# A hybrid attention and state-space layer on one core: two more pairs of gate blocks by Strassen's rule, other filler places, later loads, and low weight parts by ScalarE and an adding DMA

## The chip, the cores and the metric

The kernel runs on one core of a Trainium2 chip. The metric is the device time of one execution in microseconds (us). Before the change the median of three runs is 1958.16 us (1956.68 to 1961.07).

## What is computed

One layer of a streaming encoder is applied to 1152 tokens: a prompt of 1024 and eight samples of 16. One wide input projection feeds two branches, and what matters here is this part of it:

```python
h = rms_norm(x, norm_g) * (1 + scale) + shift
proj = h @ w_in
q, k, v, z_att, z_ssd, xbc, dt_raw, gates = jnp.split(proj, IN_SPLITS, axis=-1)
...
y = (y + d_skip.astype(jnp.float32)[:, None] * xs_h).reshape(b, s, SSD_WIDTH).astype(x.dtype)
y = y * jax.nn.silu(z_ssd)
...
merged = jax.nn.sigmoid(g_att) * att_branch + jax.nn.sigmoid(g_ssd) * ssd_branch
out = x + gate * (merged @ w_out)
```

`z_ssd` has 2048 columns, that is 16 blocks of 128, one for each pair of state-space heads. `gates` has 16 blocks, `xbc` 24. The state-space scan (`ssd_scan`) works on 32 heads in four groups, in chunks.

## The kernel before

All products with weights are made in fp32r as three matmuls: a weight block is split into a high part (ScalarE copies it to fp32r, L372) and a low part (VectorE subtracts the high part from the raw block, L373), and `high*high + high*low + low*high` is accumulated (L487, L488, L490). One "dense block" is 128 output columns over 1024 inputs and 1152 tokens: 8 x 3 x 3 = 72 matmuls of 128x384. `dense` (L455) does one; its three token groups are evicted from PSUM one after the other, the first two out of the two buffers `d`, the third out of `s`. Each block's two parts take two of four slots in `rarena`, so the parts of block i+1 can be written once block i-1 is done. The raw weights come by a DMA on SyncE's queue (L348) into two raw slots.

The program has these stages, all on TensorE:

- the start: loads, modulation and norm, then the first dense blocks;
- Strassen: ten of the 16 z blocks are taken two at a time (`pairs`, L823). Two output blocks over two token halves and two input halves need seven products instead of eight: per pair 7 x 4 x 2 x 3 = 168 matmuls of 128x288 (L878, L880, L881). `NPR` = 5 is the number of pairs. The results go to DRAM (`z_d`);
- attention, eight units;
- the state-space stage: 24 convolution blocks of `xbc` (`conv_gen`, L1495), 11 other dense blocks between them (the fillers: five z blocks in the pairs 3, 5, 9, 11, 13, three gate blocks in the groups 1 to 3, three in the pairs 7, 14, 15), the scan of 16 pairs of heads (`ssd`, L1665), and six more gate blocks at its end (`gates_dense`);
- the tail: attention projection, state-space projection, output projection.

In the state-space stage the order of the instructions is made at build time by generators: `dense` blocks are issued while the steps of the scan are paced between them by a clock that the program keeps for itself. For pair p, `prelude` (L1708) loads the decays of its two heads (`acs_d`, two broadcasts of 576 KB), the exponentials `eacs_d` (two of 288 KB, into `eb`) and the state `h0`, and ScalarE turns the decays into masks (L1728, L1732). `main` (L1738) transposes x (L1755), makes the states (L1800), the output within the chunks (L1828, L1835) and from the states (L1856), multiplies by `eb` (L1861) and by z (L1869), and stores y through GpSimd's queue (L1873). A z block made early comes back from `z_d` in `main` (L1841). One that is made in the stage lies in SBUF from its eviction (L1698 on ScalarE, L1699 on VectorE) to L1869. The engines work in order; GpSimd's queue has the stores of the stage, memsets and copies for the convolution (L1498, L1501, L1517, L1518) and masks (L1789).

Of the kernel before, what the change touches and what calls it, by code (L numbers as in the profile page):

```python
# [18 lines left out]
NT = NP + NB * NS  # L19
G3 = NT // 3  # L20
NH = 16
HD = 64
NU = NH // 2
NPAIR = 16
NG = 4
PPG = NPAIR // NG
# [103 lines left out]
def trunk_kernel(ctx: ExitStack, tc: tile.TileContext, h):  # L130
    nc = tc.nc
# [4 lines left out]
    drp = ctx.enter_context(tc.tile_pool(name="drp", bufs=1, space=bass.MemoryType.DRAM))  # L136
# [30 lines left out]
    class Slots:  # L167
# [12 lines left out]
        def alloc(self, dtype):  # L180
            return Slot(self, self.free.pop(0), dtype)
# [35 lines left out]
    for n, w in PARAMS:  # L217
# [31 lines left out]
    L_SSD = marena.set_layout(Z0, [("X", 1, XW), ("R", 2, 1184), ("t", 8, 36), ("pad", 1, 576), ("T", 9, NT), ("Y", 1, 1184), ("H", 1, 1024),  # L249
                                  ("g", 3, G3)])  # L250
# [62 lines left out]
    store = nc.gpsimd.dma_start  # L313
# [8 lines left out]
    z_d = drp.tile([1 + len(EARLY), P, NT], F32, name="z_d")  # L322

    def rsqrt_small(v):

# [9 lines left out]
    jobs, parts = [], []  # L335
# [16 lines left out]
    def w_split(i, keep=lambda x: x, cold=None):  # L352

        n = len(jobs[i])
        if n == 2:
            raise NoSlot("pair")
        if n == 4:
            return w_split_last(i, keep)
        if i not in wsplit:
            lay = L_W3 if n == 3 else L_WA if jobs_att[0] <= i <= jobs_att[1] else L_W  # L360
            hi = alloc(lay, "w", n * 1024, cold)
            try:
                lo = alloc(lay, "w", n * 1024, cold)
# [8 lines left out]
        keep(nc.scalar.activation(hi.r[:, c], b.ap, AF.Copy))  # L372
        keep(nc.vector.tensor_tensor(lo.r[:, c], b.ap, hi.ap[:, c], ALU.subtract))  # L373
        b.free()
        wsplit[i][2] = j + 1
        w_ahead()
# [631 lines left out]

    def keep_block(n, z):
        what, i = AHEAD_BLOCKS[n - 1]  # L1010
        dma(gate_d[i] if what == "gate" else z_d[1 + EARLY.index(i)], z.ap)

    z = [alloc(L_VT, "T", NT)]
    w_done(0)
# [597 lines left out]

    ngate = [4]

    def gate_dense(**how):
        i = ngate[0]
        ngate[0] += 1

        def ev(o, g, tok, ps):
            t = yield from walloc(L_SSD, "g", G3)  # L1620
            nc.scalar.activation(t.ap, ps, AF.Tanh, scale=0.5)
            store(gate_d[i][:, tok], t.ap)
            stored(t)

        yield from dense(hops, ev, **how)
# [4 lines left out]
    def group_dense(g, lay):  # L1630
        res = grp[g] = {"b": [], "c": [], "sq": None, "st": None}
        yield from conv_gen(16 + g, lay, res["b"])
        if g:
            yield from gate_dense()
        yield from conv_gen(20 + g, lay, res["c"])

    def group_lat(g):
# [30 lines left out]
    def ssd(p):  # L1668
# [10 lines left out]
        def dense_gen():  # L1679
            res = st["x"] = []  # L1680
            lay = L_SSD if p else L_HEAD
            while p > AHEAD and not ssd_all[p - AHEAD]:
                blocked[0] = "pairs ahead"
                yield None
            if p % PPG:
                yield from conv_gen(p, lay, res)
            if p in EARLY:
                st["go"] = True
                if p % PPG == 0:
                    yield from conv_gen(p, lay, res)  # L1690
                if p in GATED:
                    yield from gate_dense()
                return
            z = yield from walloc(lay, "T", NT)
            st["go"] = True

            def evz(o, g_, tok, ps):
                nc.scalar.activation(z.ap[:, tok], ps, AF.Tanh, scale=0.5)  # L1698
                nc.vector.scalar_tensor_tensor(z.ap[:, tok], z.ap[:, tok], 1.0, ps, ALU.add, ALU.mult)  # L1699

            yield from dense(hops, evz)
            if p % PPG == 0:
                yield from conv_gen(p, lay, res)
            st["z"] = z
            if p in GATED:
                yield from gate_dense()

        def prelude():  # L1708

            yield from ready(lambda: "go" in st and "t" in dts and ssd_all[p] and "cbm" in grp[g])  # L1710
            res = grp[g]
            yield from until(dts["t"])
            me = []
            for hd in hds:
                a = yield from walloc(lay, "T", NT)
                dma(a.ap, acs_d[hd:hd + 1].to_broadcast([P, NT]))
                me.append(a)
            eb = yield from walloc(lay, "T", NT)
            for e in range(2):
                dma(eb.ap[e * HD:(e + 1) * HD], eacs_d[hds[e]:hds[e] + 1].to_broadcast([HD, NT]))  # L1720
            h0 = yield from walloc(lay, "H", NP)
            dma(h0.ap, h["h0"][p])
            yield from pause(7000)
            for e in range(2):

                for c in range(9):
                    cs = slice(c * P, (c + 1) * P)
                    nc.scalar.activation(me[e].ap[:, cs], me[e].ap[:, cs], AF.Relu, scale=-1.0,  # L1728
                                         bias=a4[:, c, hds[e]:hds[e] + 1])
                    if c % 3 == 2:  # L1730
                        yield from pause(1100)
                nc.scalar.activation(me[e].ap, me[e].ap, AF.Exp, scale=-1.0)  # L1732
# [3 lines left out]
            st["me"] = me, eb, h0, clock[0] + 1500  # L1736

        def main():  # L1738
            yield from ready(lambda: ssd_all[p] and ("z" in st or p in EARLY) and "cbm" in grp[g] and "t" in dts and st.get("x"))
            x, tx = st["x"][0]  # L1740
            res = grp[g]
            tokb, ct = res["tok"], res["ct"]
# [19 lines left out]
            me, eb, h0, tm = st["me"]  # L1762
            ssd_all[p + 1] = True

            if res["st"] is None:
# [73 lines left out]
            if p in EARLY:  # L1839
                z = alloc(lay, "T", NT)  # L1840
                dma(z.ap, z_d[1 + EARLY.index(p)])  # L1841
# [371 lines left out]
```

## Time and profile before

| what | value |
|---|---|
| median of three runs | 1958.16 us |
| profiled execution, its own time | 1957.76 us |
| its span, first to last instruction | 1955.9 us |
| VectorE busy | 1231.6 us, 63% |
| ScalarE busy | 794.4 us, 41% |
| GpSimd busy | 328.2 us, 17% |
| mean granted TensorE clock | 0.998 |

Times of the profile are of one execution. The windows view gives, for a stretch of it, how long each engine was busy and how many instructions it began. A matmul is pipelined, so TensorE can read as busy without a gap while matmuls begin twice as often as they last; what one costs is the stretch divided by its count. The waits view tells which engine sat idle before which line, and what ended that.

### The profile page before, as it was taken

To read this page: it belongs to the slowest core of one execution; us is meant where nothing else is said; L and a number is where in the kernel's file an instruction comes from. 1 tells how busy PE (TensorE), PEld (TensorE's weight loads), DVE (VectorE), ACT (ScalarE), POOL (GpSimd) and SP (SyncE) were. 2 spreads that over 40 slices of the span, in tenths; PEclk is the share of its full clock that TensorE was granted. 3 is DMA by queue.
4 is the path that set the end of the run, shared out by engine and by line. 5 is a ranking of instruction groups with operands and counts; after the bars stand their busy time and mean duration, and the time that the engine had idled before them with its cause. 6 is when DMAs were issued, how large, how long until landed. Compare 5 with 4: busy or idle time off the path is not lost. (4 is left out here: it accounts for less than half of the span.)

```text
span 1955.9 us, 35553 instructions
## 1 busy us (share of the span) xinstructions
PE 1931.8 (99%) x14211; PEld 1848.8 (95%) x14211; DVE 1231.6 (63%) x2545; ACT 794.4 (41%) x1627; POOL 328.2 (17%) x612
## 2 busy tenths in 40 slices
PE   7999999999999999999999999999999999999999
PEld 5999999998999998989999999989999999999999
DVE  7756346556555564585968768987775434777732
ACT  8433244444444444456545544655333301111200
POOL 0000032131231212210223322322322300000000
PEclk9999999999999999999999999999999999999999
DMA  8223423333333323234444444564357653331241
GB/s 317 88 80 105 178 68 94 128 115 96 122 103 113 121 95 117 80 121 118 129 132 131 147 129 148 155 187 147 93 177 271 234 192 92 104 104 56 84 144 53
DMA packets 84477, 252.82 MB, mean 129 GB/s; under 512 B 14540, under 2 KB 15576, under 8 KB 84312
## 3 DMA queue, kind: packets, MB, share of 16 engines
q1 hardware_dynamic: 76120, 224.26, 35.8%
q0 software_dynamic: 8192, 26.29, 3.5%
q8 instruction: 112, 1.84, 0.4%
q14 instruction: 53, 0.43, 0.1%
HBM read 199.78 MB, written 50.73 MB: 128 GB/s over the span
## 5 line engine op out<-in xcount | busy, mean ns | idle before, releaser
L487 PE MATMUL d<-rarena 128*128 128x384 f32 x1352 | 462.8, 342 | 5.7 <-DVE ma_att L1699 2.8
L490 PE MATMUL d<-rarena 128*128 128x384 f32 x1352 | 456.1, 337 | 0.0
L488 PE MATMUL d<-rarena 128*128 128x384 f32 x1352 | 455.7, 337 | 0.0
L487 PEld LDWEIGHTS d<-rarena 128*128 128x128 f32 x1352 | 254.8, 188 | 11.5 <-issue 3.7
L488 PEld LDWEIGHTS d<-rarena 128*128 128x128 f32 x1352 | 255.0, 189 | 1.2 <-issue 0.7
L490 PEld LDWEIGHTS d<-rarena 128*128 128x128 f32 x1352 | 254.6, 188 | 1.4 <-issue 1.1
L555 PE MATMUL d<-va_att,rarena 128*128 128x384 f32 (+1 forms) x567 | 197.6, 349 | 0.0
L553 PE MATMUL d<-va_att,rarena 128*128 128x384 f32 (+1 forms) x567 | 196.6, 347 | 0.0
L554 PE MATMUL d<-va_att,rarena 128*128 128x384 f32 (+1 forms) x567 | 193.7, 342 | 0.0
L372 ACT ACTIVATE rarena<-arena 128x1024 fp32r<-128x1024 f32 x80 | 84.7, 1059 | 268.0 <-PE s L488 175.7
L487 PE MATMUL s<-rarena 128*128 128x384 f32 x520 | 176.9, 340 | 0.0
L488 PE MATMUL s<-rarena 128*128 128x384 f32 x520 | 174.6, 336 | 0.0
L490 PE MATMUL s<-rarena 128*128 128x384 f32 x520 | 174.2, 335 | 0.0
L1297 ACT ACTIVATE ma_att<-ma_att 128x640 f32<-128x640 f32 (+2 forms) x144 | 101.5, 706 | 136.9 <-DVE ma_att L1406 99.7
L373 DVE TENSOR_TENSOR rarena<-arena,rarena 128x1024 fp32r<-128x1024 f32 x80 | 98.8, 1235 | 51.5 <-ACT rarena L372 51.3
L1226 POOL TENSOR_SCALAR ma_att<-ma_att 128x16 f32<-128x16 f32 (+1 forms) x24 | 5.2, 216 | 665.5 <-DVE ma_att L1203 664.8
L555 PEld LDWEIGHTS d<-va_att,rarena 128*128 128x128 f32 x567 | 107.1, 189 | 3.9 <-issue 2.7
L553 PEld LDWEIGHTS d<-va_att,rarena 128*128 128x128 f32 x567 | 106.8, 188 | 2.7 <-issue 1.2
L554 PEld LDWEIGHTS d<-va_att,rarena 128*128 128x128 f32 x567 | 106.8, 188 | 0.5
L487 PEld LDWEIGHTS s<-rarena 128*128 128x128 f32 x520 | 97.7, 188 | 2.2 <-issue 1.8
L1529 DVE SCALAR_TENSOR_TENSOR ma_att<-ma_att,arena 128x1176 f32<-128x1176 f32 x63 | 94.3, 1496 | 6.4 <-ACT ma_att L1526 5.9
L488 PEld LDWEIGHTS s<-rarena 128*128 128x128 f32 x520 | 97.7, 188 | 0.0
(436 smaller groups left out, 3914.9 us busy)
## 6 DMA issues: line engine op xcount, KB each, us to landing
arena<-in_wall_dram SPq DMA_DIRECT2D x85, 512.0 KB, 3.8
ma_att<-in_kc_dram SPq DMA_DIRECT2D x64, 256.0 KB, 4.5
ma_att<-in_vc_dram SPq DMA_DIRECT2D x64, 256.0 KB, 3.2
ma_att<-acs_d SPq DMA_DIRECT2D x26, 576.0 KB, 4.0
y_d<-ma_att POOLq DMA_DIRECT2D x15, 576.0 KB, 3.4
ma_att<-y_d SPq DMA_DIRECT2D x15, 576.0 KB, 4.8
arena<-in_wssd_dram SPq DMA_DIRECT2D x16, 512.0 KB, 4.5
ma_att<-eacs_d SPq DMA_DIRECT2D x24, 288.0 KB, 5.6
```

What stands on the lines that cost most here:

```text
L372: keep(nc.scalar.activation(hi.r[:, c], b.ap, AF.Copy))
L373: keep(nc.vector.tensor_tensor(lo.r[:, c], b.ap, hi.ap[:, c], ALU.subtract))
L487: nc.tensor.matmul(ps, hi.r[:, wc], kh.r[:, tok], start=k == 0, stop=False)
L488: nc.tensor.matmul(ps, hi.r[:, wc], kl.r[:, tok], start=False, stop=False)
L490: nc.tensor.matmul(ps, lo.r[:, wc], kh.r[:, tok], start=False, stop=k == nk - 1)
L553: nc.tensor.matmul(ps, kh.r[:, tok], wh, start=j == 0, stop=False)
L554: nc.tensor.matmul(ps, kh.r[:, tok], wl, start=False, stop=False)
L555: nc.tensor.matmul(ps, kl.r[:, tok], wh, start=False, stop=j == KT - 1)
L1226: nc.gpsimd.tensor_scalar(ss, ss, 1.0 / HD, EPS, ALU.mult, ALU.add)
L1297: nc.scalar.activation(p, p, AF.Exp, bias=sm_[:, 4 + e:5 + e], scale=-1.0, accum_out=sm_[:, 6 + e:7 + e])
L1529: nc.vector.scalar_tensor_tensor(yc, r.ap[:, j:j + n], w4[:, i, j:j + 1], yc, ALU.mult, ALU.add)
```

## The change

1. `NPR` goes from 5 to 7. Fourteen of the 16 z blocks (0 to 13) go by Strassen's rule, z block 14 is one dense block right after them (before, z block 15 was); all z now go through DRAM.
2. The fillers of the state-space stage are seven instead of eleven: z block 15 in pair 1, gate blocks in the pairs 3, 6, 9, 11, 13 and 15. `fill_dense` makes them; the groups have none. Six gate blocks stay at the stage's end.
3. `eb` is no longer loaded in `prelude` but in `main`, after the output within the chunks; z is loaded right behind it, for every pair. VectorE's multiplications wait for them (`until(te)`, `until(tz)`).
4. For the weight blocks of the state-space stage (from the first convolution block to the last gate block) the low part is made without VectorE: ScalarE writes the negated high part into the low slot (L375 of the changed file), and a DMA on GpSimd's queue adds the raw block from DRAM to it (L376). The blocks of the other stages go as before.

```diff
-GATED = (7, 14, 15)
-NGATE = 7 + len(GATED)
-EARLY = tuple(p for p in range(16) if p not in (3, 5, 9, 11, 13))
-AHEAD_BLOCKS = [("gate", i) for i in range(4)] + [("z", p) for p in EARLY]
+NEARLY = 15
+SLOTS = (('p', 1), ('p', 3), ('p', 6), ('p', 9), ('p', 11), ('p', 13), ('p', 15))
+AHEAD_BLOCKS = [("gate", i) for i in range(4)] + [("z", p) for p in range(NEARLY)]
...
-NPR = 5
+NPR = 7
...
         keep(nc.scalar.activation(hi.r[:, c], b.ap, AF.Copy))
-        keep(nc.vector.tensor_tensor(lo.r[:, c], b.ap, hi.ap[:, c], ALU.subtract))
+        if jobs_att[1] <= i < len(jobs) - 32:
+            keep(nc.scalar.activation(lo.r[:, c], hi.ap[:, c], AF.Copy, scale=-1.0))
+            keep(nc.gpsimd.dma_start(lo.r[:, c], parts[jobs[i][j]], accum_op=ALU.add))
+        else:
+            keep(nc.vector.tensor_tensor(lo.r[:, c], b.ap, hi.ap[:, c], ALU.subtract))
...
+    def fill_dense(*slot):
+        what, i = FILL[slot]
+        if what == "gate":
+            yield from gate_dense()
+            return
+
+        def ev(o, g, tok, ps):
+            t = yield from walloc(L_SSD, "g", G3)
+            nc.scalar.activation(t.ap, ps, AF.Tanh, scale=0.5)
+            nc.vector.scalar_tensor_tensor(t.ap, t.ap, 1.0, ps, ALU.add, ALU.mult)
+            store(z_d[1 + i][:, tok], t.ap)
+            stored(t)
+
+        yield from dense(hops, ev)
...
-            eb = yield from walloc(lay, "T", NT)
-            for e in range(2):
-                dma(eb.ap[e * HD:(e + 1) * HD], eacs_d[hds[e]:hds[e] + 1].to_broadcast([HD, NT]))
             h0 = yield from walloc(lay, "H", NP)
...
-            if p in EARLY:
-                z = alloc(lay, "T", NT)
-                dma(z.ap, z_d[1 + EARLY.index(p)])
-                tz = clock[0] + 6500
-            else:
-                z, tz = st["z"], 0.0
+            eb = alloc(lay, "T", NT)
+            for e in range(2):
+                dma(eb.ap[e * HD:(e + 1) * HD], eacs_d[hds[e]:hds[e] + 1].to_broadcast([HD, NT]))
+            z = alloc(lay, "T", NT)
+            dma(z.ap, z_d[1 + p])
+            te, tz = clock[0] + 6500, clock[0] + 8500
...
+                yield from until(te)
                 nc.vector.tensor_tensor(eb.ap[:, c2], eb.ap[:, c2], v, ALU.mult)
```

Three queues show what moves in the state-space stage. First ScalarE, before, in the middle of the stage: L372 is the high part of a weight block, L1506, L1509 and L1510 are the evictions of a convolution block, L1621 of a gate block, L1728 and L1732 the masks out of the decays.

```order
L1728 ACTIVATE ma_att<-ma_att 128x128 x18
L1732 ACTIVATE ma_att<-ma_att 128x1152 x2
L372 ACTIVATE rarena<-arena 128x1024
L1509 ACTIVATE ma_att<-s_13324 128x256
L1510 ACTIVATE ma_att<-s_13324 128x8x16
L1526 ACTIVATE ma_att<-ma_att,arena 128x1176
L1621 ACTIVATE ma_att<-d_13358 128x384
```

ScalarE in the changed kernel, at a like place (L373 is the high part, L375 the negated copy, L1511 the eviction of a convolution block, L1730 and L1734 the masks):

```order
L373 ACTIVATE rarena<-arena 128x1024
L1734 ACTIVATE ma_att<-ma_att 128x1152 x2
L1531 ACTIVATE ma_att<-ma_att,arena 128x1176
L1511 ACTIVATE ma_att<-d_13078 128x384
L1783 ACTIVATE rarena<-ma_att 64x128
L1730 ACTIVATE ma_att<-ma_att 128x128
L375 ACTIVATE rarena<-rarena 128x1024
L1730 ACTIVATE ma_att<-ma_att 128x128 x7
L1877 ACTIVATE va_ssd<-ma_att 128x1152
```

The negated copy is new, and it does not always follow its high part at once: here an eviction of the block that is running and a mask on a decay stand between the two. In most blocks one or two instructions do.

Next GpSimd's queue before, late in the stage (L1815 and L1899 store states, L1873 y, L1789 makes masks for the samples' state):

```order
L1498 MEMSET ma_att 128x3
L1501 COPY ma_att<-ma_att 128x8x3
L1815 DMA out_hp_dram<-ma_att 128x128
L1789 TENSOR_TENSOR rarena<-rarena,arena 128x256 x2
L1873 DMA y_d<-ma_att 128x1152
L1498 MEMSET ma_att 128x3
L1501 COPY ma_att<-ma_att 128x8x3
L1899 DMA out_hs_dram<-ma_att 128x1024
```

And in the changed kernel (L376 is the adding DMA, L1522 to L1524 the tails of a convolution block, L1876 stores y, L1902 the samples' states, L1817 the prompt's state):

```order
L376 DMA rarena<-in_wall_dram 128x1024
L1876 DMA y_d<-ma_att 128x1152
L1503 MEMSET ma_att 128x3
L1791 TENSOR_TENSOR rarena<-rarena,arena 128x256 x2
L1902 DMA out_hs_dram<-qa_ssd 128x1024
L1817 DMA out_hp_dram<-ma_att 128x128
L1522 COPY ma_att<-ma_att 128x3
L1523 COPY ma_att<-ma_att 128x24
L1524 DMA out_conv_dram<-ma_att 128x27
L376 DMA rarena<-in_wall_dram 128x1024
```

The adding DMA stands once per weight block in this queue, behind whatever is queued there, and mostly right behind the copies that follow the end of a convolution block; there are 34 of them.

Last SyncE's queue before, around one pair of heads (L1716 loads decays, L1720 `eb`, L1722 `h0`, L1841 z, L348 raw weights):

```order
L1722 DMA qa_ssd<-in_h_dram 128x1024
L1716 DMA ma_att<-acs_d 128x1152 x2
L1720 DMA ma_att<-eacs_d 64x1152 x2
L348 DMA arena<-in_wall_dram 128x1024
L1716 DMA ma_att<-acs_d 128x1152 x2
L1722 DMA ma_att<-in_h_dram 128x1024
L1720 DMA ma_att<-eacs_d 64x1152
L1841 DMA va_ssd<-z_d 128x1152
```

And in the changed kernel (L1721 loads decays, L1843 `eb`, L1724 `h0`, L1845 z, L349 raw weights):

```order
L1724 DMA ma_att<-in_h_dram 128x1024
L1721 DMA ma_att<-acs_d 128x1152
L349 DMA arena<-in_wall_dram 128x1024
L1843 DMA va_ssd<-eacs_d 64x1152 x2
L1845 DMA ma_att<-z_d 128x1152
L1721 DMA ma_att<-acs_d 128x1152
```

The loads of `eb` are now beside that of z, and the second of the two decays of a pair stands behind both.

More of the change, by code (lines that the diff above doesn't have):

```diff
@@ L31 @@
 AHEAD = 2
-GATED = (7, 14, 15)
-NGATE = 7 + len(GATED)
-EARLY = tuple(p for p in range(16) if p not in (3, 5, 9, 11, 13))
-AHEAD_BLOCKS = [("gate", i) for i in range(4)] + [("z", p) for p in EARLY]
+NEARLY = 15
+SLOTS = (('p', 1), ('p', 3), ('p', 6), ('p', 9), ('p', 11), ('p', 13), ('p', 15))
+AHEAD_BLOCKS = [("gate", i) for i in range(4)] + [("z", p) for p in range(NEARLY)]
+FILL = dict(zip(SLOTS, [("z", p) for p in range(NEARLY, NPAIR)] + [("gate", 4 + i) for i in range(len(SLOTS) - NPAIR + NEARLY)]))
+NGATE = 4 + len(SLOTS) - NPAIR + NEARLY
 NZ = 5
-NPR = 5
+NPR = 7
 TH = NT // 2
@@ L321, in trunk_kernel @@
     gate_d = drp.tile([16, P, NT], F32, name="gate_d")
-    z_d = drp.tile([1 + len(EARLY), P, NT], F32, name="z_d")
+    z_d = drp.tile([1 + NPAIR, P, NT], F32, name="z_d")
     def rsqrt_small(v):
@@ L1010, in keep_block @@
         what, i = AHEAD_BLOCKS[n - 1]
-        dma(gate_d[i] if what == "gate" else z_d[1 + EARLY.index(i)], z.ap)
+        dma(gate_d[i] if what == "gate" else z_d[1 + i], z.ap)
     z = [alloc(L_VT, "T", NT)]
@@ L1632, in group_dense @@
         yield from conv_gen(16 + g, lay, res["b"])
-        if g:
-            yield from gate_dense()
+        if ("g", g) in FILL:
+            yield from fill_dense("g", g)
         yield from conv_gen(20 + g, lay, res["c"])
@@ L1686, in dense_gen @@
                 yield from conv_gen(p, lay, res)
-            if p in EARLY:
[L1688 to L1694, printed above, removed]
             st["go"] = True
[L1697 to L1701, printed above, removed]
             if p % PPG == 0:
                 yield from conv_gen(p, lay, res)
-            st["z"] = z
-            if p in GATED:
-                yield from gate_dense()
+            if ("p", p) in FILL:
+                yield from fill_dense("p", p)
         def prelude():
@@ L1735, in prelude @@
                 yield from pause(1000)
-            st["me"] = me, eb, h0, clock[0] + 1500
+            st["me"] = me, h0, clock[0] + 1500
         def main():
-            yield from ready(lambda: ssd_all[p] and ("z" in st or p in EARLY) and "cbm" in grp[g] and "t" in dts and st.get("x"))
+            yield from ready(lambda: ssd_all[p] and "cbm" in grp[g] and "t" in dts and st.get("x"))
             x, tx = st["x"][0]
@@ L1761, in main @@
             yield from ready(lambda: "me" in st)
-            me, eb, h0, tm = st["me"]
+            me, h0, tm = st["me"]
             ssd_all[p + 1] = True
@@ L2115, with fill @@
             ar["wlast"] = lay(b.reshape(P, 4, 2 * NQL).transpose(1, 0, 2))
-    order, gate = [], 4
+    order = []
+    def fill(*slot):
+        if slot in FILL:
+            what, i = FILL[slot]
+            order.append((ga if what == "gate" else zs) + i * P)
     for g in range(NG):
         order.append(xb + 2048 + g * P)
-        if g:
-            order.append(ga + gate * P)
-            gate += 1
+        fill("g", g)
         order.append(xb + 2560 + g * P)
-        for j in range(PPG):
-            p = g * PPG + j
-            order += [xb + p * P] if p in EARLY else [xb + p * P, zs + p * P][::1 if j else -1]
-            if p in GATED:
-                order.append(ga + gate * P)
-                gate += 1
-    order += [ga + i * P for i in range(gate, 16)]
+        for p in range(g * PPG, g * PPG + PPG):
+            order.append(xb + p * P)
+            fill("p", p)
+    order += [ga + i * P for i in range(NGATE, 16)]
     ar["wall"] = lay(np.stack(first + [kblock(wi, o, P) for o in order]))
```

1 line of the change is left out of this document (removed).

## The prediction

> **What bounds the kernel now.** I read the page first, then TensorE's waits, then stretches of the program, and last the lines that the change touches. The page's engine row and two of its slice rows:
>
> ```profile
> PE 1931.8 (99%) x14211; PEld 1848.8 (95%) x14211; DVE 1231.6 (63%) x2545; ACT 794.4 (41%) x1627; POOL 328.2 (17%) x612
> PE   7999999999999999999999999999999999999999
> DVE  7756346556555564585968768987775434777732
> ```
>
> TensorE is busy from end to end; the others have room, VectorE least, in slices 18 to 28, the state-space stage. TensorE's waits, all of them:
>
> ```profile
> PE g L632 <- DMA m<-in_xT_dram: 8.9, 3, 8.3
> PE d L487 <- DVE ma_att L1699: 2.8, 1, 2.8
> PE d L487 <- DVE ma_att L998: 2.8, 1, 2.8
> PE g L1755 <- DVE ma_att L1535: 2.6, 1, 2.6
> PE g L1828 <- DVE ma_att L1809: 1.0, 1, 1.0
> PE s L720 <- ACT rarena L701: 0.9, 1, 0.9
> PE s L720 <- DVE rarena L713: 0.9, 1, 0.9
> PE d L748 <- DVE arena L739: 0.4, 1, 0.4
> ```
>
> The first lies in the start, L998 before the state-space stage; 2.8, 2.6 and 1.0 lie in it, 6.4 us. "Busy" says little of a pipelined engine, so I count what a matmul costs, in stretches that hold one kind: the Strassen stage, the state-space stage as a whole, and 100 us of dense work in the tail.
>
> ```profile
> 100.90:213.00 112.10, 112.10 (x844) 112.10 (x843) 65.24 (x114) 35.54 (x69) 0.00 (x0) 1.00 0.30 100
> 885.00:1571.00 686.00, 679.60 (x5094) 661.97 (x5093) 507.99 (x859) 330.19 (x674) 173.15 (x298) 1.00 0.50 160
> 1700.00:1800.00 100.00, 100.00 (x579) 100.00 (x578) 78.45 (x120) 17.63 (x16) 0.00 (x0) 1.00 0.25 78
> ```
>
> The columns behind the length are TensorE, weight loads, VectorE, ScalarE and GpSimd, then granted clock, DMA share and GB/s. A dense matmul costs 100 / 579 = 0.1727 us, a Strassen one 112.1 / 844 = 0.1328 us. The clock is 1.00 in all three, so nothing is to be had there. So: TensorE's work sets the end, and time can come only out of that work or out of its few waits.
>
> **The change, part by part.**
>
> *Two more Strassen pairs.* Four dense blocks leave, all fillers of the state-space stage: 4 x 72 x 0.1727 = 49.7 us. Two pairs come: 2 x 168 x 0.1328 = 44.6 us. Sum -5.1 us. The Strassen stage has VectorE at 65 of 112 us and ScalarE at 36, and no wait of TensorE lies in it; a longer stage of the same kind should go as fast. The sum holds only if TensorE stays the bound in the stage that loses work. There the other engines' shares become: VectorE 508 - 34 x 1.2 (low parts) - 4 x (1.2 + 3 x 0.55) (split and evictions of the z blocks that leave) = 456 of 636 us; ScalarE 330 + 34 x 1.06 - 4 x (1.06 + 3 x 0.48) = 356 of 636. The durations (minimum/median/maximum in ns) are from these rows, the first of the state-space stage alone, and the 34 from the order of GpSimd's queue:
>
> ```profile
> L372 ACT ACTIVATE rarena<-arena x40: 1038/1058/1067, 895.1 to 1559.3; 128x1024 fp32r<-128x1024 f32 x40
> L373 DVE TENSOR_TENSOR rarena<-arena,rarena x80: 1210/1225/1629, 72.5 to 1928.3; 128x1024 fp32r<-128x1024 f32 x80
> L1698 ACT ACTIVATE ma_att<-d x10: 468/485/495, 967.7 to 1384.3; 128x384 f32<-128x384 f32 x10
> L1699 DVE SCALAR_TENSOR_TENSOR ma_att<-ma_att,d x10: 541/547/553, 969.2 to 1387.9; 128x384 f32<-128x384 f32 x10
> ```
>
> VectorE is at 74% now and would be at 72% of a shorter stage. No engine becomes the bound by its sum.
>
> *The stage's present waits.* What stands behind the 2.8 us at L1699 is on ScalarE:
>
> ```profile
> 1283.66 2.75 ACT L1728 ACTIVATE ma_att<-ma_att 128x128 f32<-128x128 f32 x9 [4.22 <-DMA ma_att<-acs_d]
> 1287.19 2.75 ACT L1728 ACTIVATE ma_att<-ma_att 128x128 f32<-128x128 f32 x9 [0.78 <-DMA ma_att<-acs_d]
> 1289.85 1.15 ACT L1732 ACTIVATE ma_att<-ma_att 128x1152 f32<-128x1152 f32 x1
> 1290.90 0.47 ACT L1698 ACTIVATE ma_att<-d 128x384 f32<-128x384 f32 x1
> ```
>
> The decays came late, the masks waited for them, and the z block's eviction was queued behind the masks. That z block is gone, and a gate block's eviction has no VectorE step; I take the 2.8 us off. The 2.6 us stand before the first pair's transposes, which the order of TensorE now puts a third of a dense block later: I take half, 1.3, and leave the 1.0. So -4.1 us, between 0 and -6.4.
>
> *The adding DMA.* It replaces a subtraction that came out of VectorE at once by a negated copy (1.06 us), a queue and a transfer. TensorE needs the low part when a block's third matmul begins. Slots are free when the block before is done, so there is one block's length, at least 12.4 us, for all of it. No adding transfer is in this trace. The nearest rows are GpSimd's stores of the same 512 KB and the loads of the raw weights, from issue to landing (min/median/max), with the stores' issue:
>
> ```profile
> L1899 POOL DMA_DIRECT2D out_hs_dram<-ma_att x8: 531/537/580, 996.1 to 1527.2; - x8
> DMA to landing us min/median/max: 2.9/3.4/7.4
> ...
> DMA to landing us min/median/max: 3.2/4.0/7.2
> ```
>
> It reads both its source and its destination. From below it costs one store, 3.4 us; from above a load and a store one after the other at their slowest and median, 7.4 + 4.0 = 11.4. I take 5.0, nearer to the store, which is the same size on the same queue. Most copies start as the slots come free; then the part is there after 1.06 + 1.06 + 5.0 = 7.1 us, or about 8 with an instruction between the copies, of 12.4 or more. A late one:
>
> ```profile
> 1474.87 0.33 PE L487 MATMUL d<-rarena 128*128 128x384 f32 x1
> 1480.10 1.05 ACT L372 ACTIVATE rarena<-arena 128x1024 fp32r<-128x1024 f32 x1
> 1482.31 1.22 DVE L373 TENSOR_TENSOR rarena<-arena,rarena 128x1024 fp32r<-128x1024 f32 x1
> 1488.66 0.33 PE L490 MATMUL d<-rarena 128*128 128x384 f32 x1
> ```
>
> Its block began at 1474.87, its high copy only at 1480.10, behind masks, and the next block's L490 came at 1488.66. With the change its low part would land at 1480.10 + 1.05 + 1.06 + 5.0 = 1487.2, in time; at 7.4 us it lands at 1489.6, 0.9 us late; at 11.4 at 1493.6, 4.9 late. I suppose 8 such blocks of 34 (an estimate: by these rows 16 + 1 + 1 = 18 of the stage's 40 high copies waited for TensorE and so were not late, and of the other 22 I take a third):
>
> ```profile
>   PE s L488: 40.3, 16
>   PE g L488: 8.8, 1
>   PE g L1388: 2.4, 1
> ```
>
> I book 8 x 0.45 = +3.6 us, half-way between 0 and 0.9 each; the ends are 0 and 8 x 4.9 = 39. GpSimd's queue also matters: the DMA waits behind copies and stores in order, but these wait for things that end with the block before.
>
> The Trainium skill speaks against this part (SBUF — State Buffer, section "A bandwidth-pool intuition that's wrong"): a DMA whose descriptors GpSimd writes took about 3.1 us instead of 0.62 beside a copy on VectorE that holds the port they share. The stores above, issued with VectorE busy three quarters of the time, show an issue of 531 to 580 ns, so this trace shows no such stall at issue, though landings up to 7.4 could hold one. By that rule each transfer would take 2.5 us more than the 5.0 that I take, and the sum would be about 1957.6, as at the low end of the first rival.
>
> *Late loads of `eb`.* VectorE now waits for `eb` in order; the transposes' results and states are queued behind it, and TensorE waits for those. The rows for its load from issue to landing, for the late z loads, and for z's wait so far:
>
> ```profile
> DMA to landing us min/median/max: 4.7/5.6/6.6
> ...
> L1841 SPq DMA_DIRECT2D va_ssd<-z_d x7: 320/327/536, 953.6 to 1395.9; - x7
> L1841 SPq DMA_DIRECT2D ma_att<-z_d x4: 320/326/383, 1025.8 to 1482.4; - x4
>   DVE ma_att L1869: 1.4, 1
> ```
>
> It is needed after the skip term, with 6.5 us allowed in the program. Landing 5.6 to 6.6 fits barely, and z beside it takes bandwidth. The 7 + 4 late z loads cost VectorE one wait of 1.4 us. I book +1.0 us on TensorE; below: a gain of 2 if the decays, freed of `eb` before them, come sooner; above: see the second rival.
>
> *Sum*, on the profiled execution (span 1955.9, its own time 1957.76, 0.4 below the median of 1958.16): 1957.8 - 5.1 - 4.1 + 3.6 + 1.0 = **1953.2 us**.
>
> **The rivals.**
>
> *Low parts come late (slower).* Mechanism: the adding transfer takes longer than a store, at L490 of each late block TensorE waits. It decides from a landing of about 6.5 us on. Midway between 7.4 and 11.4, at 9.4, a late block waits 2.9 us: 8 x 2.9 = 23, and 1957.8 - 5.1 - 4.1 + 23 + 1 = 1973 us. At 7.5 it is 8 x 1.0 and 1957.6; at 11.4 it is 39 and 1989. For it: the transfer reads twice, and DMA engines are at half their time in this stage already (0.50). Against: most blocks in the stage are longer than 12.4, 686 / 40 = 17 us from one high copy to the next. Chance 0.17.
>
> *Waits on decays and `eb` take the gain back (no change).* ScalarE serves both the masks and the evictions of dense blocks, and its waits for decays are long:
>
> ```profile
> ACT ma_att L1728 <- DMA ma_att<-acs_d: 48.5, 15, 8.4
> ACT va_ssd L1728 <- DMA va_ssd<-acs_d: 25.5, 5, 8.0
> ```
>
> The second decay of a pair now stands in SyncE's queue behind `eb` and z. So far 20 such waits cost TensorE one of 2.8 us. If one of the 16 pairs still costs that, the sum is 1957.8 - 5.1 - 1.3 + 3.6 + 2.8 = 1957.8; with three it is 1963. I put it at 1958. Chance 0.17.
>
> *The stage does not shorten.* If the chain of one pair to the next sets the pace, not TensorE, the four blocks that leave give nothing: 1957.8 + 44.6 = 2002 us. Against: 6.4 us of waits in 686, and engine sums of 72% and less. Chance 0.04.
>
> **How the numbers follow.** The forecast's case has 0.62. What can be told from no change is 0.2%, 3.9 us: faster is below 1954.2, slower above 1962.1. Within the forecast's case the waits may vanish (1957.8 - 5.1 - 6.4 = 1946) or grow by a few us; 0.53 of its 0.62 are below 1954.2, 0.09 within. The second rival gives 0.14 to the same and 0.03 to slower, the first 0.03 to the same and 0.14 to slower, the third 0.04 to slower: 0.53 / 0.26 / 0.21. The range starts at 1946 and goes to 1968, which leaves out the upper half of the first rival and the third, about 0.15.
>
> **What would show it.** Right: the Strassen stage 44.6 us longer at 0.133 us a matmul; the state-space stage about 50 us shorter; no wait at the changed file's third matmul line (L495) for the adding DMA, whose landing is near 5 us; L1699's wait gone. Wrong: TensorE waiting at L495 some 3 us per late block (first rival); ScalarE's waits for `acs_d` longer than 74 us in all with TensorE waiting for evictions or transposes behind them (second); the state-space stage still near 686 us (third). The forecast is wrong too if TensorE's waits in that stage come to more than 10 us for any other reason.

## The result and the profile after

The changed kernel takes 1974.6 us (median of 6 runs, 1972.3 to 1979.7) against 1958.4 us for the kernel before (6 runs, 1956.7 to 1963.3): ratio 1.0086, 95% interval 1.0069 to 1.0102. It is slower by 16 us; 1953.2 was forecast, with a range up to 1968. Its profiled execution has a span of 1976.3 us, 20.4 more than before.

The stretches come first, as before: the Strassen stage and the state-space stage of the kernel after (length, TensorE, weight loads, VectorE, ScalarE, GpSimd, granted clock, DMA share, GB/s).

```profile
100.90:257.70 156.80, 156.80 (x1179) 156.80 (x1178) 92.63 (x161) 49.75 (x97) 0.00 (x0) 1.00 0.29 100
930.00:1591.50 661.50, 638.76 (x4806) 621.22 (x4805) 456.66 (x806) 350.40 (x690) 189.92 (x334) 0.98 0.67 195
```

The Strassen stage grew by 156.8 - 112.1 = 44.7 us, as forecast. The state-space stage shrank by 686.0 - 661.5 = 24.5 us only, where 49.7 us of matmuls had left it; 44.7 - 24.5 = 20.2 is nearly the whole difference of the spans, 20.4. In that stage TensorE is now idle for 661.5 - 638.8 = 22.7 us (6.4 before), its granted clock is 0.98 (1.00 before), and the DMA engines' share has risen from 0.50 to 0.67. TensorE's longest waits in that stage (us in total, times, longest):

```profile
PE g L1858 <- DVE ma_att L1851: 4.5, 1, 4.5
PE g L1802 <- DVE va_ssd L1761: 4.3, 1, 4.3
PE g L1858 <- DVE va_ssd L1851: 3.9, 1, 3.9
PE g L1858 <- DVE ma_att L1864: 3.5, 1, 3.5
PE d L495 <- DMA rarena<-in_wall_dram: 2.7, 1, 2.7
```

Once in 34 blocks TensorE waits for a low part (L495): that adding DMA was issued late, behind other work of GpSimd, and landed after 5.6 us. The other four are single stalls of 3.5 to 4.5 us before the scan's own matmuls, behind VectorE. The chain of waits that ends in the first of them, in the stretch from 1398 us on (start, us, what):

```profile
1398.74 7.27 DMA out_hs_dram<-ma_att
1406.01 0.02 SPq L1724
...
1407.08 3.23 DMA ya<-va_ssd
...
1410.45 5.93 DMA va_ssd<-acs_d
...
1416.48 2.75 ACT va_ssd L1730 x9
1419.25 1.17 ACT va_ssd L1734
1420.44 1.36 DVE va_ssd L1736
...
1422.82 0.67 DVE ma_att L1851
1423.48 0.04 issue
1423.53 1.65 PE g L1858 x6
```

Read downwards: a store of samples' states, issued right behind an adding DMA, takes 7.27 us to land (the median of these stores was 3.4 before and is 5.6 now; the slowest took 7.4 already before); only then may SyncE's queue load `h0` into the freed buffer, behind which stand a small store (`ya`, 3.23 us) and, behind that, the decays; these take 5.93 us; then the masks, then TensorE. The stall at 1032 us ends a shorter chain, of which this is the middle:

```profile
1022.28 8.96 DMA ma_att<-eacs_d
1031.25 0.03 issue
1031.28 0.05 DVEq L1864
```

The late `eb` landed after 8.96 us where the order allows 6.5; an adding DMA was issued 3 us into its way. VectorE used it 9.6 us after its first half was issued; in the first experiment below, without adding DMAs, 6.0 us. The stall at 1483 us ends a chain with a store of y:

```profile
1473.50 8.22 DMA y_d<-va_ssd
...
1481.84 1.30 DVE va_ssd L1761 x2
```

This store was issued before the next adding DMA of its queue (1474.61 us), so it was not held up by standing behind it. The fourth stall, 3.9 us at 1172 us, has a store of y (6.41 us) and a load of decays (4.07) behind it, and it isn't new with the adding DMAs: the first experiment below, without them, has it with 3.3 us (4.12 and 7.21).

What the stalls cost beyond their own length shows in 20 us stretches around the waits of 3.9, 2.7 and 4.5 us, and in TensorE's timeline behind the last of these:

```profile
1160.00:1180.00 20.00, 16.13 (x134) 15.49 (x133) 13.06 (x25) 9.94 (x24) 3.17 (x6) 0.83 0.81 243
1300.00:1320.00 20.00, 19.59 (x140) 18.51 (x140) 15.56 (x28) 6.96 (x10) 3.77 (x9) 0.84 0.62 182
1420.00:1440.00 20.00, 16.47 (x86) 16.47 (x87) 11.72 (x20) 12.75 (x35) 5.86 (x14) 0.83 0.58 180
```

```profile
1427.64 0.52 PE L492 MATMUL d<-rarena 128*128 128x384 f32 x1
1427.96 0.52 PE L493 MATMUL d<-rarena 128*128 128x384 f32 x1
...
1430.04 0.34 PE L492 MATMUL s<-rarena 128*128 128x384 f32 x1
1430.22 0.34 PE L493 MATMUL s<-rarena 128*128 128x384 f32 x1
```

After the stall a dense matmul begins every 0.32 us until about 1429, then every 0.18. So a stall is paid twice: once as idle time, once as slow matmuls that the waits view doesn't list.

The rows of the adding DMA (issue in ns, minimum/median/maximum, and time to landing) and of GpSimd's DMA queue (packets, MB, share of 16 engines):

```profile
L376 POOL DMA_DIRECT2D rarena<-in_wall_dram x34: 892/914/1077, 872.1 to 1543.4; - x34
...
DMA to landing us min/median/max: 5.4/7.0/10.7
```

```profile
q0 software_dynamic: 13280, 44.71, 8.9%
```

Its median landing is 7.0 us, above the 5.0 that was taken and the 6.5 from which the first rival decided, and inside the bounds of 3.4 and 11.4. Even so nearly all low parts came in time.

### The profile page after: what moved, and what is told of

Read it like the earlier page. It is cut to its first block, busy times and chain, and to the rows that moved or that the text cites. A ratio compares the mean times of both kernels' runs of the same rounds, so it can differ in the third digit from the quotient of the medians.

```text
span 1976.3 us, 35824 instructions
## 1 busy us (share of the span) xinstructions
PE 1936.0 (98%) x14259; PEld 1853.1 (94%) x14259; DVE 1208.4 (61%) x2543; ACT 830.1 (42%) x1673; POOL 344.6 (17%) x649
## 4 chain that ended last, share of the span: by engine, by line
PE 88%; DMA 6%; ACT 2%; issue 2%; DVE 1%; POOL 1%; SPq 0%; POOLq 0%; DVEq 0%; ACTq 0%
PE d L492 10%; PE d L495 10%; PE d L493 10%; PE d L560 5%; PE d L558 5%; PE d L559 5%; PE s L492 4%; PE s L493 4%; PE s L495 4%; PE g L1314 3%; PE g L1337 3%; PE s L1393 2%; PE g L883 2%; PE g L886 2%; PE g L885 2%
## 5 line engine op out<-in xcount | busy, mean ns | idle before, releaser
L492 PE MATMUL d<-rarena 128*128 128x384 f32 x1288 | 441.9, 343 | 2.9 <-DVE ma_att L1003 2.9
L495 PE MATMUL d<-rarena 128*128 128x384 f32 x1288 | 436.9, 339 | 2.7 <-DMA rarena<-in_wall_dram 2.7
L493 PE MATMUL d<-rarena 128*128 128x384 f32 x1288 | 435.7, 338 | 0.0
L492 PEld LDWEIGHTS d<-rarena 128*128 128x128 f32 x1288 | 244.3, 190 | 6.9 <-DVE ma_att L1003 3.2
L495 PEld LDWEIGHTS d<-rarena 128*128 128x128 f32 x1288 | 244.1, 190 | 3.8 <-DMA rarena<-in_wall_dram 3.0
L493 PEld LDWEIGHTS d<-rarena 128*128 128x128 f32 x1288 | 244.5, 190 | 0.5 <-issue 0.2
L373 ACT ACTIVATE rarena<-arena 128x1024 fp32r<-128x1024 f32 x76 | 80.5, 1059 | 260.4 <-PE s L493 173.9
L492 PE MATMUL s<-rarena 128*128 128x384 f32 x488 | 166.6, 341 | 0.0
L495 PE MATMUL s<-rarena 128*128 128x384 f32 x488 | 164.8, 338 | 0.0
L493 PE MATMUL s<-rarena 128*128 128x384 f32 x488 | 164.4, 337 | 0.0
L1534 DVE SCALAR_TENSOR_TENSOR ma_att<-ma_att,arena 128x1176 f32<-128x1176 f32 x63 | 93.4, 1483 | 15.4 <-ACT ma_att L1531 14.9
L492 PEld LDWEIGHTS s<-rarena 128*128 128x128 f32 x488 | 92.5, 190 | 1.9 <-issue 1.8
L495 PEld LDWEIGHTS s<-rarena 128*128 128x128 f32 x488 | 92.2, 189 | 1.0 <-issue 1.0
L493 PEld LDWEIGHTS s<-rarena 128*128 128x128 f32 x488 | 92.4, 189 | 0.2 <-issue 0.2
```

Source lines behind the costliest of these rows:

```text
L492: nc.tensor.matmul(ps, hi.r[:, wc], kh.r[:, tok], start=k == 0, stop=False)
L493: nc.tensor.matmul(ps, hi.r[:, wc], kl.r[:, tok], start=False, stop=False)
L495: nc.tensor.matmul(ps, lo.r[:, wc], kh.r[:, tok], start=False, stop=k == nk - 1)
L1534: nc.vector.scalar_tensor_tensor(yc, r.ap[:, j:j + n], w4[:, i, j:j + 1], yc, ALU.mult, ALU.add)
```

## The experiments

**Theory 1**: the adding DMAs take the DMA engines' time, so the loads (decays, `eb`) and stores that share these engines land late, and engines whose queues run in order stall TensorE. **Theory 2**: `eb`, and the second decay behind it, land late because the change asks for them late. **Rivals within theory 1**: that the cost lies in TensorE or a buffer waiting for the low part, or in ScalarE's second copy. Except where it is said otherwise, each is an edit of the kernel after. The state-space stage is read from 930 us on (885 in edits of the kernel before) to 384.8 us ahead of the end of the span, the length of the tail.

**The low parts by VectorE again.**

```
-        if jobs_att[1] <= i < len(jobs) - 32:
+        if False:
```

> The changed kernel with the low parts made by VectorE's subtraction again; everything else as changed. Theory 1 (the adding DMAs load the DMA engines: 34 of them raised GpSimd's queue from 3.5% to 8.9% of 16 engines' span, 3.2 us of all 16 engines each, and so decays, eb and stores land late): TensorE's waits in the state-space stage fall from 22 to about 6 us, time 1950 to 1957. Theory 2 (the late loads of eb and of the second decay land late by themselves): the waits before L1858 and L1802 stay, time 1968 to 1977.

Measured: 1948.73 us, ratio to the kernel before 0.9962 (0.9947 to 0.9977). Without the adding DMA the rest of the change is a gain, a little larger than theory 1 expected. Its stage, its longest wait there, and GpSimd's queue:

```profile
930.00:1565.80 635.80, 628.34 (x4804) 611.92 (x4803) 495.83 (x842) 320.84 (x657) 172.19 (x301) 1.00 0.54 175
```

```profile
PE g L1858 <- DVE va_ssd L1851: 3.3, 1, 3.3
```

```profile
q0 software_dynamic: 8384, 26.88, 3.5%
```

The stage is 686.0 - 635.8 = 50.2 us shorter than before, what the four blocks are worth. Against it the kernel after is 25.7 us longer: 22.7 - 7.5 = 15.2 us of it idle and 638.8 - 628.3 = 10.4 us busy for the same matmuls (4806 and 4804), that is, the clock. And GpSimd's queue gives the price of one adding DMA: (8.9% x 1976.3 - 3.5% x 1950.6) / 34 = 3.2 us of all 16 DMA engines.

**The adding DMA alone**, put into the kernel before (the two lines of L375 and L376 in place of the subtraction, in its state-space stage: 38 blocks, as four z blocks more are made there).

> The kernel before, with only the low parts of the state-space weights by negated copy and adding DMA. Theory 1: loads land late here too, time 1966 to 1978, 8 us or more above before. Theory 2: nothing that matters, 1953 to 1962.

Measured: 1970.05 us, ratio 1.0065 (1.0048 to 1.0082), the stage 702.0 us with 14.8 us idle against 686.0 and 6.4. So it costs 1970.0 - 1956.7 = 13 us there, half of the 26 it costs in the kernel after, though there are 38 of them. Here TensorE did wait for low parts, 7.5 us in three times.

**`eb` loaded in the prelude again**: the first of these lines comes back there, with the two loads, and the others, with their loads, leave `main`; z is then due after 6.5 us in place of 8.5, as before.

```
+            eb = yield from walloc(lay, "T", NT)
...
-            eb = alloc(lay, "T", NT)
...
-                yield from until(te)
```

> The changed kernel with eb loaded in the prelude again, before h0, as in the kernel before; z stays late, the adding DMA stays. Theory 1: still 1966 to 1978, since the decays and stores stay late. Theory 2: the waits before L1858 go, 1950 to 1958.

Measured: 1991.61 us, ratio 1.0175 (1.016 to 1.019); the size missed both expectations. The late load isn't the culprit: without it the kernel is 17 us slower still, and low parts come late (L495 waits 10.1 us in six times). Theory 2 falls.

**A plain DMA without the addition** (the low part is then the whole weight block).

```
-            keep(nc.gpsimd.dma_start(lo.r[:, c], parts[jobs[i][j]], accum_op=ALU.add))
+            keep(nc.gpsimd.dma_start(lo.r[:, c], parts[jobs[i][j]]))
```

> The changed kernel with the DMA that makes the low part a plain one, without the addition: it overwrites the negated high part with the raw weight (so the low part is the whole weight and the state-space results are not those of the reference); same queue, size and waits. Theory 1, if the price is in the addition: GpSimd's queue falls to about 6%, landing from 7.0 to about 4 us, time 1954 to 1963. Theory 1, if the price is in the bytes alone, and theory 2: time 1968 to 1977.

Measured: 1967.32 us, ratio 1.005 (1.0034 to 1.0066), between the expectations. Stage, queue, and the DMA's issue:

```profile
930.00:1580.90 650.90, 632.82 (x4807) 615.80 (x4806) 455.92 (x806) 351.00 (x690) 182.92 (x334) 0.99 0.62 198
```

```profile
q0 software_dynamic: 13280, 44.71, 6.8%
```

```profile
L376 POOL DMA_DIRECT2D rarena<-in_wall_dram x34: 542/548/760, 872.3 to 1532.8; - x34
```

A plain load of the same bytes takes (6.8% x 1965.7 - 68.3) / 34 = 1.9 us of the 16 engines and gives back 7 of the 26 us.

**Both parts undone**, the low parts by VectorE and `eb` early (the first and the third edit together).

> The kernel after with two parts undone: the low parts by VectorE's subtraction again and `eb` loaded in the prelude again. With the run that undid the first part alone (1948.7 us) and the one that undid the second alone (1991.6) it fills the square of the two. If the two parts work by themselves, undoing both gives 1948.7 + (1991.6 - 1974.6) = 1966 (1960 to 1972). If the early `eb` only hurts because the adding DMAs make its loads land late, it costs little without them: 1947 to 1955.

Measured: 1967.52 us, ratio 1.0048 (1.0033 to 1.0064): 18.8 us more than with the late `eb`, with or without adding DMAs about the same price, so the two parts add up (1966 was expected for that case). Read the other way, the adding DMAs cost 1991.6 - 1967.5 = 24 us with the early `eb` too. What waits there are other lines than in the kernel after, all at the stage's end (1536 to 1575 us):

```profile
PE g L492 <- ACT rarena L1929: 6.0, 2, 3.6
PE g L1883 <- DVE va_ssd L1863: 3.8, 1, 3.8
PE g L1145 <- DVE va_ssd L1898: 3.0, 1, 3.0
```

**The low parts by GpSimd's subtraction.**

```
+            keep(nc.gpsimd.tensor_tensor(lo.r[:, c], b.ap, hi.ap[:, c], ALU.subtract))
```

> The kernel after with the low parts of the same blocks subtracted by GpSimd: no negated copy by ScalarE, no adding DMA, and VectorE relieved as in the kernel after. If VectorE's relief is worth something and the load on the DMA engines is what spoils it, 1940 to 1950, at or below the 1948.7 with VectorE's subtraction. If GpSimd is too slow for it, or its work slows VectorE, the low parts come late or VectorE's chains do: 1952 to 1985.

Measured: 1953.84 us, ratio 0.9974 (0.9963 to 0.9985): faster than before, and 5 us behind VectorE's subtraction. Its stage, and the subtraction:

```profile
930.00:1570.20 640.20, 629.66 (x4804) 613.21 (x4803) 494.36 (x809) 321.09 (x657) 258.37 (x334) 0.99 0.54 174
```

```profile
L375 POOL TENSOR_TENSOR rarena<-arena,rarena x34: 2369/2400/3617, 868.8 to 1520.7; 128x1024 fp32r<-128x1024 f32 x34
```

VectorE isn't relieved: it is busy for 494.4 us with 809 instructions, where the kernel after needs 456.7 for 806.

**Bytes that nobody waits for, first try**: VectorE's subtraction, and beside it a plain DMA from the weight to a place in DRAM.

```
+            nc.gpsimd.dma_start(dummy_d[len(jobs) - 33 - i, :, c], parts[jobs[i][j]])
```

> The kernel after with the low parts by VectorE's subtraction, and beside each of them a plain DMA of the same 512 KB on GpSimd's queue, from the weight in DRAM to a place in DRAM that nobody reads: the bytes without anyone waiting for them, and without ScalarE's negated copy. If the bytes on the DMA engines are the cost, the chains of decays, `eb` and stores are late again: 1958 to 1970, with stalls of TensorE behind L1864, L1851 or L1761 of 3 to 5 us. If the cost lies in ScalarE's second copy or in the low part waiting for its DMA, 1947 to 1954.

Measured: 2005.67 us, ratio 1.0241 (1.0223 to 1.0259), and it doesn't test what it was made for: as the transfers depend on nothing, they were all issued in the first 54 us of the program, in front of and among the first inputs.

```profile
PE g L638 <- DMA m<-in_xT_dram: 54.5, 6, 22.4
```

That is 46 us more than the 8.9 before, most of the 57 us over the run without these transfers; the state-space stage was left without them. The second try below ties them to the block's high part.

**ScalarE's negated copy kept, the weight added by VectorE.**

```
-            keep(nc.gpsimd.dma_start(lo.r[:, c], parts[jobs[i][j]], accum_op=ALU.add))
+            keep(nc.vector.tensor_tensor(lo.r[:, c], b.ap, lo.ap[:, c], ALU.add))
```

> The kernel after with ScalarE's negated copy kept and the weight added to it by VectorE in place of the DMA: the price of the second copy alone, in the same places of the queues. If the transfers are the cost, 1948 to 1955 (the copies are 34 x about 1 us on a ScalarE that is half idle). If ScalarE's second copy delays its masks and evictions enough to matter, 1958 to 1970.

Measured: 1948.33 us, ratio 0.9953 (0.9938 to 0.9968).

```profile
930.00:1561.40 631.40, 627.90 (x4807) 610.81 (x4806) 497.33 (x843) 350.43 (x691) 167.03 (x301) 1.00 0.54 176
```

The second copy costs nothing that can be measured (1948.3 against 1948.7), with ScalarE as busy as in the kernel after. All of the 26 us lie in the DMA.

**An adding DMA that nobody waits for**: VectorE's subtraction, and in the adding DMA's place one that adds the high part to one place in DRAM.

```
+            keep(nc.gpsimd.dma_start(dummy_d, hi.ap[:, c], accum_op=ALU.add))
```

> The kernel after with the low parts by VectorE's subtraction, and beside each a DMA of 512 KB on GpSimd's queue in the adding DMA's place: it adds the block's high part (SBUF) to one place in DRAM that nobody reads (the first of them stores it). No engine waits for any of them. If the adding transfers on the DMA engines are what costs, the loads and stores behind them are late again: 1962 to 1978, the DMA share of the state-space stage near 0.65 and TensorE idle in it 15 to 25 us. If the cost lies in the low part or its buffer waiting for the DMA, 1947 to 1954 with some 5 to 8 us idle.

Measured: 1971.6 us, ratio 1.0073 (1.0053 to 1.0092). Stage, waits, queue:

```profile
930.00:1583.50 653.50, 633.54 (x4813) 616.63 (x4812) 494.22 (x847) 321.64 (x661) 200.97 (x336) 0.99 0.67 197
```

```profile
PE g L1863 <- DVE ma_att L1856: 6.1, 1, 6.1
PE g L1683 <- DVE ma_att L1545: 3.4, 1, 3.4
PE g L1863 <- DVE ma_att L1869: 3.2, 2, 1.9
PE g L1807 <- DVE va_ssd L1766: 2.5, 1, 2.5
```

```profile
q0 software_dynamic: 13280, 44.71, 9.0%
```

Three of these are the lines that stall in the kernel after (L1856, L1869 and L1766 here are L1851, L1864 and L1761 there), with the same DMA share, and the trace shows no engine waiting for any of the new transfers. So a load of this kind costs 23 us, against the 26 of the kernel after, without a low part that waits for it.

**Plain stores that nobody waits for** (the same line without `accum_op`).

> The same with plain stores of the high part, every one of them: a lighter load on the DMA engines (a 512 KB store took about 1.4 us of all 16 engines against 3.2 for an adding DMA). If the cost goes with the time that the DMA engines are taken, 1952 to 1964, between 1948.7 (none) and the adding ones; if waiting for the low part is the cost, 1947 to 1954.

Measured: 1955.37 us, ratio 0.9992 (0.9982 to 1.0001), 7 us above none; the DMA share of the stage is 0.60 and TensorE is idle for 8.1 us of it. GpSimd's queue has 5.9% of the engines' span, so a plain store took (5.9% x 1953.5 - 68.3) / 34 = 1.4 us of the 16 engines.

```profile
930.00:1568.70 638.70, 630.60 (x4815) 614.46 (x4814) 496.27 (x847) 321.94 (x663) 192.83 (x336) 0.99 0.60 202
```

**The adding DMA for every second block**: one kernel with `and i % 2`, and later one with `and i % 2 == 0`, in the condition; the other blocks have VectorE's subtraction. By the bytes of GpSimd's queue these are 16 and 18 of the 34.

> The kernel after with the adding DMA for every second block of the stage alone, VectorE's subtraction for the others: 17 adding DMAs in place of 34. If the cost goes with the load in a straight line, half of the 26 us is gone: 1957 to 1966. If a few stalls at fixed places make it (chains of loads that just miss), it is either near 1949 to 1953 or still 1968 to 1976.

> The adding DMA for the other half of the stage's blocks alone. If chains at fixed places miss their times with any load in front of them, this half costs about as much as the first: 1966 to 1976. If the first half holds the blocks that matter, little: 1949 to 1957. In a straight line: 1957 to 1966.

Measured: 1971.3 us (ratio 1.0069, 1.0054 to 1.0085) for the 16 and 1959.43 us (1.0014, 1.0001 to 1.0026) for the 18.

```profile
930.00:1583.20 653.20, 634.26 (x4803) 615.56 (x4802) 478.34 (x826) 334.99 (x673) 181.30 (x317) 0.99 0.60 183
```

```profile
930.00:1569.20 639.20, 630.14 (x4811) 613.93 (x4810) 477.53 (x825) 335.45 (x674) 178.91 (x318) 0.99 0.62 188
```

The first row is of the 16, the second of the 18. The 16 cost 23 us and the 18 cost 11, at about the same load: the first time fits a few stalls at fixed places, the second a straight line, and so it matters which transfer is delayed, not only how many there are. With the 16, the longest waits are these:

```profile
PE g L1884 <- POOL rarena L1791: 6.0, 2, 4.8
PE g L1858 <- DVE va_ssd L1851: 5.7, 1, 5.7
```

The first is a path that the kernel after doesn't show among its longest: GpSimd's masks (L1791) came late, behind small operations of GpSimd that had stood 11.2 us before a small load (`ya`).

**`eb` late in the kernel before**, that part of the change alone; z is then due after 8.5 us in place of 6.5.

> The kernel before with one part of the change alone: `eb` loaded in the main part, beside the late z, with its wait, in place of the prelude. The runs with and without the early `eb` on the kernel after differ by 17 to 19 us, so if the late load helps by itself (a buffer less held through the prelude, a load less ahead of the decays), the kernel before gains 4 to 15 us: 1942 to 1954. If it only helps where every z block comes back through DRAM as well, 1954 to 1962.

Measured: 1959.49 us, ratio 1.0005 (0.9995 to 1.0014), nothing. The late load is worth 17 to 19 us only among the other parts of the change.

**Later due times**: the readers of decays, `eb` and z placed 3 us later, with the adding DMAs, and without them (the weight added by VectorE).

```
-            yield from pause(7000)
+            yield from pause(10000)
-            te, tz = clock[0] + 6500, clock[0] + 8500
+            te, tz = clock[0] + 9500, clock[0] + 11500
```

> The kernel after with all adding DMAs, and the due times by which the order places the readers of decays, `eb` and z 3 us later (7.0, 6.5 and 8.5 us become 10.0, 9.5 and 11.5). If the cost is that loads land later than the order expects, so that engines whose queues run in order stand behind them, much of the 26 us comes back: 1950 to 1966, with stalls behind L1851, L1864 and L1761 gone or halved. If the transfers cost TensorE in another way, 1970 to 1982.

> The same later due times without the adding DMAs (the weight added by VectorE), the control: where the loads already land in time, waiting longer for them brings nothing: 1946 to 1956 (1948.3 with the due times as they were). If the later due times help by themselves, below 1946.

Measured: 1987.85 us (ratio 1.0162, 1.0141 to 1.0183) and 1972.93 us (1.0073, 1.0052 to 1.0095). Both miss: the later order alone costs 25 us, so it is no remedy, and it doesn't show what it was to show. Under it the adding DMAs cost 15 us.

## Why the prediction was wrong, point by point

*Two more Strassen pairs*, -49.7 + 44.6: right. The Strassen stage grew by 44.7 us, and without the adding DMA the state-space stage shrank by 50.2.

*The stage's present waits*, -4.1: wrong by about 5 us. L1699's wait is gone, but with VectorE's subtraction the stage has 7.5 us of idle time in place of 6.4. One wait left and others, 3.3 us behind L1851 above all, came.

*The adding DMA*, +3.6: this is the step that failed. The runs put it at 26 us (1974.6 against 1948.7; 24 if each is taken against the kernel before measured beside it). I asked only whether the low part would be there at L495. It nearly always was: one wait of 2.7 us, less than I had booked. The price is paid by others. Each adding DMA takes the 16 DMA engines for 3.2 us, 34 of them for 108 us, nearly all in a stage of 661 us in which these engines were half busy already, and what stands behind is a store that frees a buffer, a decay, an `eb`. The bound that I took from a store's and a load's time to landing bounds this transfer's own latency, not what it does to its neighbours. That the price is in the transfers is shown: an adding one that no engine waits for costs 23 us, a plain store that no engine waits for 7, a plain load in its place 19, ScalarE's copy nothing. GpSimd's longer issue (0.91 us against 0.55) can't be the most of it, since the plain load, issued in 0.55, still costs 19. The price is not in proportion to the DMA engines' time (1.4, 1.9 and 3.2 us each cost 7, 19 and 23 to 26 us), and that late stores and loads carry it is read from the chains of single stalls.

The rule that I weighed (the Trainium skill, SBUF — State Buffer, section "A bandwidth-pool intuition that's wrong") does not explain it: it speaks of a transfer from GpSimd held up at issue beside VectorE's copies, and the issue took 0.91 us in place of 0.54, but in the run without the addition it took 0.55 beside the same VectorE. The longer issue goes with the addition.

*Late loads of `eb`*, +1.0: wrong in sign and size on this kernel, where undoing it costs 17 to 19 us, and right on the kernel before, where it gives nothing. Why the early load is so dear with all z in DRAM isn't settled; its stalls stand at the end of the stage.

*The clock*, at which I looked once ("nothing to be had there"): 10.4 of the 25.7 us in the stage are slow matmuls after stalls. I had priced a stall at its own length; here it cost about 1.7 times that (25.7 / 15.2).

*The rivals.* The first gave 1973 us, near the result, by the wrong mechanism: low parts seldom came late. The second named the right place, waits on decays and `eb`, and a price far too low (1958 to 1963), as it had no load behind it; ScalarE's waits for `acs_d`, by which I meant to know it, came to 60.1 + 11.4 = 71.5 us and not above 74, as these rows of the kernel after show:

```profile
ACT ma_att L1730 <- DMA ma_att<-acs_d: 60.1, 16, 9.1
...
ACT va_ssd L1730 <- DMA va_ssd<-acs_d: 11.4, 4, 6.2
```

The third is out, since the stage did shorten in the run without the adding DMA. The sign that I listed last did come: TensorE's waits in the stage beyond 10 us, for another reason.

*How it adds up.* Without the adding DMA the change gives -8.0 us (1948.7 against 1956.7); the adding DMA alone in the kernel before +13.4. Together they would be +5.4, and 16 was measured: the other 11 us come from having both. The late `eb` loads don't explain them, since with the early `eb` the adding DMAs still cost 24 us; what is left, the late z loads and the new places of the fillers among it, was not tried by itself. Left open, too, is which of the first half's 16 transfers are the ones that matter.

The version that beats both kernels is the change without its adding DMA: 1948.7 us with VectorE's subtraction, 1948.3 with the negated copy and VectorE's addition.

## What to carry to other kernels

Price a transfer not only by whether its own reader gets it in time but by the DMA engines' time that it takes, and look up what is queued on those engines in that stage, above all stores whose landing frees a buffer for the next load. Where TensorE is the bound, price a stall of some microseconds above its own length, because the clock can fall with it. An idle engine's help (ScalarE's copy here) is free only if the rest of its path is.

## What the runs showed of the hardware

- An adding DMA of 512 KB from DRAM into SBUF took 3.2 us of all 16 DMA engines, one from SBUF into DRAM 3.2 as well ((9.0% x 1968.3 - 68.3) / 34), a plain load on the same queue 1.9. Its issue took GpSimd 0.91 us against 0.55 for the plain one.
- Waits of TensorE of 3.9 and 4.5 us (at 1172 and 1424 us) go with a granted clock of 0.83 in their 20 us stretches, and one of 2.7 us (at 1300 us) with 0.84. In the kernel before, a wait of 2.6 us (at 936 us) goes with 0.91 from 925 to 945 us and one of 2.8 us (at 1293 us) with 1.00 from 1290 to 1310, so the length of a wait alone does not decide. The Trainium skill (TensorE: Matmul & The Clock Gate, section "Why this matters for your kernels") warns of idle gaps above about 3 us; here two shorter ones were enough and a third was not.
- GpSimd's subtraction of 128x1024 took 2.40 us, 82 us for 34 of them, and VectorE's other work took 38 us longer beside it (494.4 against 456.7). The Trainium skill (GPSIMD Engine Reference, section "Specifications", row on SBUF interfaces) says that GpSimd shares these with VectorE and contends with VectorE instructions that have two SBUF inputs; the two busy times agree with it.
